# A hybrid attention and delta-rule layer: loads of the delta rule move from GpSimd's queue to SyncE's, and its first projection is issued earlier

## The chip, the cores and the metric

One core of a Trainium2 chip runs the whole layer. The metric is the device time of one execution in microseconds (us). TensorE is called PE, VectorE DVE, ScalarE ACT, GpSimd POOL and SyncE SP, as in the profile; SPq and POOLq are the DMA queues that SP and POOL issue to.

## What is computed

One layer with 512 tokens of width 2048. An input projection feeds two groups of heads, their outputs are joined and projected, and a squared-ReLU MLP follows. The change lies in the gated delta rule of the second group (8 heads, 128 wide). Cut to what matters:

```python
def hybrid_mixer(h, w_in, ...):
    proj = h @ w_in
    q_a, k_a, v_a, qkv_d, a_raw, b_raw, z = split(proj)
    attn_out = sliding_window_attention(q_a, k_a, v_a, sinks, rel_bias)   # 16 heads of 64
    qkv_d = silu(causal_depthwise_conv(qkv_d, conv_w))                    # width 4
    q_d, k_d = l2_normalise(...), l2_normalise(...)
    o_d = chunked_gated_delta_rule(q_d, k_d, v_d, g, beta)
    o_d = rms_norm(o_d) * silu(z)
    return concatenate([attn_out, o_d]) @ w_o

def chunked_gated_delta_rule(q, k, v, g, beta):
    G = cumsum(g)                                        # per chunk
    decay_mat = exp(where(tril, G[i] - G[j], -inf))
    A = strict_tril((k * beta) @ k.T * decay_mat)
    u, w = triangular_solve(A + eye, [v * beta, k * beta * exp(G)])
    attn_intra = (q @ k.T) * decay_mat
    # then a scan over the chunks with state S

def reference(x, ...):
    x = layer_norm(alpha * x + hybrid_mixer(x, ...))
    return layer_norm(alpha * x + relu(x @ w_up) ** 2 @ w_down)
```

## The kernel before

Matmuls are in fp32 by three products of high and low parts (`mul3`). Each weight block of 512 rows by 256 columns is a "unit": SP loads it (`raw`, 512 KB), ACT makes `hi` (L110), DVE makes `lo` (L111), and PE uses them. The class `Stream` keeps four raw buffers and two buffers of cut units, so the `hi` and `lo` of one unit can be written only when PE is done with the unit two before it.

`proj()` runs four units of 24 matmuls (128x512 each, tile `pj`) for two column blocks. After each of the 16 row blocks it calls `tick()`, which lets the oldest generator of `fronts` and the oldest of `chains` issue one more step. So the small work of attention heads and of the delta rule is spread between projection matmuls. First come K, V and four Q projections, each of which adds two `attend` chains (scores `ps_s` L507, softmax L513 to L528, transposes `ps_pt` L538, output `ps_o` L554). Then, after `while chains or fronts: tick()`, the attention's memory pool `at` is closed and the pool `ch` of the delta rule is opened.

The delta rule goes over four pairs of heads, called pairs 0 to 3 below. Each has three projections with a `front` (convolution `acc` L592, SiLU `s` L598, transposes `ps_tr` L604) and then one `delta` chain, which runs beside the projections of the next pair (beside the gate projections for pair 3). Of one `delta` chain these steps matter, each for the pair's two heads:

- `C` (L673): the row of cumulated decays, broadcast to 128 partitions by a DMA from DRAM; DVE subtracts (L675, 4 per head) and clips (L678), ACT takes the exponential (L679).
- `B` and `A` (L694, L698): DVE scales the products of keys by C.
- `tri` (L712): B is sent to DRAM; `Nb` (L721): its 16x16 diagonal blocks come back, one DMA per head and chunk of 128 tokens, each element apart in 64-byte rows.
- `bl` (L704): POOL masks B for the first level of the inversion.
- `dX`, `X` (L729, L731): DVE inverts all blocks by 15 steps of substitution; `inv` (L737) sends X to DRAM, and `D` (L742) loads the block-diagonal matrix back.
- `ps_z` (L757) and `ps_c` (L767): PE doubles the block size level by level, beginning with D and `bl`.

The tag C has two buffers, which the tile `zero` (L867, sent to `inv` once by POOL) shares. A scheduler decides each engine's final order from the order of the code and from dependences; each engine then works through its list in order, so an instruction that waits holds all that stand behind it on that engine or issuing queue.

Of the kernel before, what the change touches and what calls it, by code (L numbers as in the profile page):

```python
# [17 lines left out]
P = 128  # L18
# [20 lines left out]
LEVS = (4, 5)  # L39
# [15 lines left out]
def hymba_layer(ctx: ExitStack, tc: tile.TileContext, i, out, dbg=None):  # L55
    nc = tc.nc
# [42 lines left out]
    def mmbank(name):  # L99
        return mm.tile([P, 512], F32, tag="mm", name=name)  # L100
# [4 lines left out]
    def mul3(ps, wh, wl, xh, xl, start, stop, more=False):  # L105
        for a, b, first, last in ((wh, xh, start, False), (wh, xl, False, False), (wl, xh, False, stop)):
            nc.tensor.matmul(ps, a, b, start=first, stop=last, skip_group_check=more)  # L107
# [127 lines left out]
    def tick():  # L235
        for q in (fronts, chains):
            while q:
                try:
                    next(q[0])
                    break  # L240
                except StopIteration:
                    q.popleft()
# [34 lines left out]
    def proj(before=None, ticks=1):  # L277

        pss = [mmbank(f"pj{f}") for f in range(2)]
        for u in range(4):  # L280
            for k in range(4):
                kt = u * 4 + k
                if before is not None:
                    before(kt)
                if k == 0:
                    hi, lo = ws.get()
                for f in range(2):
                    fs = slice(f * P, (f + 1) * P)
                    mul3(pss[f], hi[:, k, fs], lo[:, k, fs], xH[kt], xL[kt],
                         kt == 0, kt == KT - 1)  # L290
                for _ in range(ticks):
                    tick()
        return pss
# [266 lines left out]
    for c in range(4):  # L560
# [2 lines left out]
            chains.append(attend(2 * c + f, qps[f]))  # L563
        tick()

    while chains or fronts:
        tick()
    pat.close()
# [4 lines left out]
    H2 = range(2)  # L573


    tri = dram.tile([2, P, TT * P], F32, name="tri")
    inv = dram.tile([2, P, TT * P], F32, name="inv")

    def diagonal(m, a, t):

        v = m[a, 0, t * P:t * P + 1]
        return bass.AP(v.tensor, v.offset, [[BS * TT * P + BS, P // BS], [TT * P, BS], [1, BS]])

    def t2(tag, name, bufs=None):
        return ch.tile([P, TT, P], F32, tag=tag, name=name, bufs=bufs)
# [76 lines left out]
    def delta(pr, st):  # L662
# [5 lines left out]
        C, A, B, DT, Dm = ([None] * 2 for _ in range(5))  # L668
        gv = grow.rearrange("(t h) c -> h t c", h=8)
        for a in H2:  # L670
            h = heads[a]
            C[a] = t2("C", "C")
            nc.gpsimd.dma_start(C[a], gv[h].partition_broadcast(P))  # L673
            for t in range(TT):
                nc.vector.scalar_tensor_tensor(out=C[a][:, t, :], in0=C[a][:, t, :],  # L675
                                               scalar=G_c[:, t, h:h + 1], in1=negm,
                                               op0=ALU.subtract, op1=ALU.add)
            nc.vector.tensor_scalar(out=C[a], in0=C[a], scalar1=0.0, scalar2=None, op0=ALU.min)  # L678
            nc.scalar.activation(C[a], C[a], AF.Exp)  # L679
        yield  # L680
        for a in H2:
            A[a], B[a] = t2("A", "A"), t2("B", "B")
            for th in range(2):
# [8 lines left out]
                for tt in range(2):  # L692
                    t = th * 2 + tt
# [8 lines left out]
        def masked(a, l):  # L702
            bl = t2("bl", "bl", 2)
            nc.gpsimd.tensor_tensor(out=bl, in0=B[a], in1=lev[l].unsqueeze(1).broadcast_to([P, TT, P]),  # L704
                                    op=ALU.mult)
            return bl
# [3 lines left out]
        nb_ = P // BS  # L710
        for a in H2:
            nc.gpsimd.dma_start(tri[a], B[a].rearrange("p t c -> p (t c)"))  # L712
        yield
        bls = [masked(a, LEVS[0]) for a in H2]
        yield
        Nb = ch.tile([2 * TT * nb_, BS, BS], F32, tag="Nb", name="Nb", bufs=1)
        X = ch.tile([2 * TT * nb_, BS, BS], F32, tag="X", name="X", bufs=1)
        for a in H2:
            for t in range(TT):
                p0 = (a * TT + t) * nb_  # L720
                nc.gpsimd.dma_start(Nb[p0:p0 + nb_], diagonal(tri, a, t))  # L721
        nc.scalar.activation(X, eyes, AF.Copy)
        yield
        yield
# [9 lines left out]
        for a in H2:  # L734
            for t in range(TT):
                p0 = (a * TT + t) * nb_
                nc.gpsimd.dma_start(diagonal(inv, a, t), X[p0:p0 + nb_])  # L737
        yield
        yield
        for a in H2:  # L740
# [8 lines left out]
        for l in LEVS:  # L749
# [11 lines left out]
            if l < 5:  # L761
                bls = [masked(a, l + 1) for a in H2]
# [40 lines left out]
        for t in range(TT):  # L803
            tok = slice(t * P, (t + 1) * P)
            pss, R = [None] * 2, [None] * 2
# [23 lines left out]
            for a in H2:  # L829
                h = heads[a]  # L830
# [41 lines left out]
    for pr in range(4):  # L872
        st = {"s2": [None] * 3, "K": [None] * 2, "V": [None] * 2,
              "ss": small.tile([P, 2, 2, TT], F32, tag="ss", name="ss")}
        for role in range(3):
            pss = proj()
            fronts.append(front(role, st, pss, pr))
            tick()
        chains.append(delta(pr, st))
# [192 lines left out]
    for n in range(4):  # L1072
        ns = slice(n * 512, (n + 1) * 512)
        pss = [mmbank(f"po{t}") for t in range(TT)]
# [455 lines left out]
```

## Time and profile before

| | |
|---|---|
| median of 3 runs | 2233.16 us (2230.01 to 2242.14) |
| the profiled execution's own time | 2244.22 us |
| its span in the profile | 2242.4 us |
| PE busy | 2167.1 us, 97% of the span |
| DVE, ACT, POOL busy | 65%, 44%, 16% |

The span is that of one execution, and 1.8 us of its own time lie outside it. Start times are counted from the span's start. The delta rule and the last attention heads lie between about 195 and 700 us; before that are the first projections, after it the output projection and the MLP, which the change leaves as they are.

### The profile page before, as it was taken

The numbers are of one execution on the slowest core, as the hardware profiler recorded it, in microseconds if no ns is written. First come the engines' busy times: TensorE is split into PE (matmuls) and PEld (weight loads), VectorE is DVE, ScalarE is ACT, GpSimd is POOL, SyncE is SP. The second block draws the span as 40 slices with busy tenths as digits, with TensorE's granted clock in tenths as the row PEclk, the third lists the DMA queues.
The fourth block names the chain that finished last, engine by engine and source line by source line (L and its number), as shares of the span: only waits on it lengthen the run. The fifth ranks groups of instructions, "written<-read, shape, count | busy, mean of one in ns | idle before, by whom it ended". The sixth has DMA issues, their size and how long they took to land.

```text
span 2242.4 us, 37213 instructions
## 1 busy us (share of the span) xinstructions
PE 2167.1 (97%) x15051; PEld 1986.3 (89%) x15051; DVE 1458.8 (65%) x2170; ACT 982.7 (44%) x1474; POOL 354.1 (16%) x435
## 2 busy tenths in 40 slices
PE   8999999899999999899999999999899999999996
PEld 6777788787888887799999999999899999999995
DVE  4355567565644347867656555668788788778787
ACT  3345325233333224555555555555444444444442
POOL 0122020312110000311121111110111211211113
PEclk9999999999999999899999999999999999999998
DMA  7322332323224231389898898886898888888862
GB/s 206 94 71 71 94 110 65 94 72 82 77 77 169 94 99 62 114 216 231 207 203 214 207 204 213 208 196 212 193 226 213 194 220 210 198 212 215 202 150 94
DMA packets 157480, 352.65 MB, mean 157 GB/s; under 512 B 16539, under 2 KB 84812, under 8 KB 154748
## 3 DMA queue, kind: packets, MB, share of 16 engines
q0 software_dynamic: 40000, 132.46, 32.9%
q1 hardware_dynamic: 117308, 217.82, 28.4%
q8 instruction: 118, 1.93, 0.3%
q14 instruction: 54, 0.44, 0.1%
HBM read 325.01 MB, written 24.66 MB: 156 GB/s over the span
## 4 chain that ended last, share of the span: by engine, by line
PE 71%; issue 12%; DMA 8%; DVE 5%; POOL 2%; ACT 2%; POOLq 0%; SPq 0%; DVEq 0%; ACTq 0%
PE b L107 42%; PE pj L107 16%; PE po L107 8%; DMA raw<-in_w_down_dram 2%; DMA hf<-hd 2%; DMA T<-in_w_down_dram 1%; DVE lo L111 1%; DMA C<-grow 1%; POOL raw L186 1%; DMA tri<-B 1%; PE ps_s L507 1%; PE ps_o L554 1%; DVE mix L1438 1%; PE ps_pt L538 1%; DMA g<-in_ln_dram 1%
## 5 line engine op out<-in xcount | busy, mean ns | idle before, releaser
L107 PE MATMUL b<-slot,hi 128*128 128x256 f32 x3584 | 654.9, 286 | 8.7 <-DVE slot L1040 3.3
L111 DVE TENSOR_TENSOR lo<-raw,hi 128x1024 fp32r<-128x1024 f32 x339 | 417.9, 1233 | 312.1 <-ACT hi L110 311.8
L110 ACT ACTIVATE hi<-raw 128x1024 fp32r<-128x1024 f32 x339 | 358.8, 1059 | 508.5 <-PE b L107 252.5
L107 PEld LDWEIGHTS b<-slot,hi 128*128 128x128 f32 x3584 | 557.6, 191 | 10.6 <-DVE slot L1040 4.1
L107 PE MATMUL b<-slot,lo 128*128 128x256 f32 x1792 | 508.6, 284 | 1.5 <-DVE lo L111 1.5
L107 PE MATMUL b<-hi,slot 128*128 128x256 f32 x2608 | 477.0, 283 | 8.9 <-ACT hi L110 8.9
L107 PE MATMUL pj<-slot,hi 128*128 128x512 f32 x1408 | 462.4, 405 | 0.0
L107 PEld LDWEIGHTS b<-hi,slot 128*128 128x128 f32 x2608 | 406.5, 189 | 9.9 <-ACT hi L110 9.9
L107 PE MATMUL b<-lo,slot 128*128 128x256 f32 x1304 | 368.5, 283 | 0.8 <-DVE lo L111 0.7
L107 PEld LDWEIGHTS b<-slot,lo 128*128 128x128 f32 x1792 | 343.1, 192 | 2.4 <-DVE lo L111 2.4
L107 PEld LDWEIGHTS pj<-slot,hi 128*128 128x128 f32 x1408 | 262.5, 191 | 61.6 <-issue 6.0
L107 PE MATMUL pj<-slot,lo 128*128 128x512 f32 x704 | 283.7, 403 | 6.3 <-DVE lo L111 6.2
L110 ACT ACTIVATE hi<-T 128x1024 fp32r<-128x1024 f32 x164 | 173.7, 1060 | 201.0 <-PE b L107 181.6
L111 DVE TENSOR_TENSOR lo<-T,hi 128x1024 fp32r<-128x1024 f32 x164 | 201.8, 1231 | 83.8 <-ACT hi L110 83.8
L107 PEld LDWEIGHTS b<-lo,slot 128*128 128x128 f32 x1304 | 246.8, 189 | 1.4 <-DVE lo L111 1.3
L1001 DVE TENSOR_TENSOR mix<-mix,b 128x512 f32<-128x512 f32 x223 | 152.8, 686 | 60.6 <-PE b L107 60.2
L107 PE MATMUL b<-hl,slot 128*128 128x256 f32 x1296 | 164.5, 283 | 4.3 <-DVE mix L1001 4.3
L107 PEld LDWEIGHTS pj<-slot,lo 128*128 128x128 f32 x704 | 133.7, 190 | 37.0 <-DVE lo L111 8.3
L107 PEld LDWEIGHTS b<-hl,slot 128*128 128x128 f32 x1296 | 158.8, 191 | 5.7 <-issue 4.1
L186 POOL DMA_DIRECT2D raw<-in_w_down_dram x90 | 77.9, 865 | 496.9 <-DVE lo L111 268.7
L1001 DVE TENSOR_TENSOR F<-F,b 128x512 f32<-128x512 f32 x144 | 99.1, 688 | 82.3 <-PE b L107 80.6
L107 PE MATMUL po<-hi,slot 128*128 128x512 f32 x448 | 141.0, 395 | 0.0
(265 smaller groups left out, 2149.8 us busy)
## 6 DMA issues: line engine op xcount, KB each, us to landing
raw<-in_w_down_dram POOLq DMA_DIRECT2D x90, 512.0 KB, 5.8
raw<-in_w_in_dram SPq DMA_DIRECT2D x88, 512.0 KB, 3.5
raw<-in_w_up_dram POOLq DMA_DIRECT2D x84, 512.0 KB, 6.1
T<-in_w_down_dram SPq DMA_DIRECT2D x60, 512.0 KB, 4.7
T<-in_w_up_dram SPq DMA_DIRECT2D x56, 512.0 KB, 4.9
raw<-in_w_up_dram SPq DMA_DIRECT2D x44, 512.0 KB, 4.3
raw<-in_w_down_dram SPq DMA_DIRECT2D x34, 512.0 KB, 4.5
raw<-in_w_o_dram SPq DMA_DIRECT2D x32, 512.0 KB, 3.6
```

The lines of the kernel that those rows point to most:

```text
L107: nc.tensor.matmul(ps, a, b, start=first, stop=last, skip_group_check=more)
L110: nc.scalar.activation(hi, src, AF.Copy)
L111: nc.vector.tensor_tensor(out=lo, in0=src, in1=hi.bitcast(F32), op=ALU.subtract)
L186: nc.gpsimd.dma_start(src, nxt_, accum_op=ALU.add)
L507: nc.tensor.matmul(sc, qT[hp, b * P:(b + 1) * P], kd[hp, e, b * P + k0 - 128:(b + 1) * P], start=True, stop=True)
L538: nc.tensor.transpose(pst[:, (bb * 2 + kk) * P:(bb * 2 + kk + 1) * P], lg[a][:, b, kk * P:(kk + 1) * P], ident)
L554: nc.tensor.matmul(pso[a * 64:(a + 1) * 64, b * P:(b + n) * P], vt[:, b, vf_, vh:vh + 64], pTf[:, (2 * b + 1) * P:(2 * b + 1 + n) * P], st ...
L1001: eng.tensor_tensor(out=dst, in0=p, in1=q, op=op)
L1438: nc.vector.tensor_tensor(out=yt, in0=yt, in1=g, op=ALU.mult)
```

## The change

Four edits. The DMA that fills C is issued by SP and no longer by POOL. So are the eight DMAs of a pair that fill Nb. The two first masks `bl` are written after the sends of `inv` instead of ahead of the Nb loads, and one `yield` goes. The first of the delta rule's projections is issued before the loop that drains the attention chains, not after it.

```diff
--- before.py
+++ after.py
@@ -563,6 +563,8 @@
             chains.append(attend(2 * c + f, qps[f]))
         tick()
 
+
+    pss0 = proj()
     while chains or fronts:
         tick()
     pat.close()
@@ -670,7 +672,7 @@
         for a in H2:
             h = heads[a]
             C[a] = t2("C", "C")
-            nc.gpsimd.dma_start(C[a], gv[h].partition_broadcast(P))
+            nc.sync.dma_start(C[a], gv[h].partition_broadcast(P))
             for t in range(TT):
                 nc.vector.scalar_tensor_tensor(out=C[a][:, t, :], in0=C[a][:, t, :],
                                                scalar=G_c[:, t, h:h + 1], in1=negm,
@@ -711,14 +713,12 @@
         for a in H2:
             nc.gpsimd.dma_start(tri[a], B[a].rearrange("p t c -> p (t c)"))
         yield
-        bls = [masked(a, LEVS[0]) for a in H2]
-        yield
         Nb = ch.tile([2 * TT * nb_, BS, BS], F32, tag="Nb", name="Nb", bufs=1)
         X = ch.tile([2 * TT * nb_, BS, BS], F32, tag="X", name="X", bufs=1)
         for a in H2:
             for t in range(TT):
                 p0 = (a * TT + t) * nb_
-                nc.gpsimd.dma_start(Nb[p0:p0 + nb_], diagonal(tri, a, t))
+                nc.sync.dma_start(Nb[p0:p0 + nb_], diagonal(tri, a, t))
         nc.scalar.activation(X, eyes, AF.Copy)
         yield
         yield
@@ -735,6 +735,7 @@
             for t in range(TT):
                 p0 = (a * TT + t) * nb_
                 nc.gpsimd.dma_start(diagonal(inv, a, t), X[p0:p0 + nb_])
+        bls = [masked(a, LEVS[0]) for a in H2]
         yield
         yield
         for a in H2:
@@ -873,7 +874,7 @@
         st = {"s2": [None] * 3, "K": [None] * 2, "V": [None] * 2,
               "ss": small.tile([P, 2, 2, TT], F32, tag="ss", name="ss")}
         for role in range(3):
-            pss = proj()
+            pss = proj() if pr or role else pss0
             fronts.append(front(role, st, pss, pr))
             tick()
         chains.append(delta(pr, st))
```

What the scheduler makes of it can be read from the order of instructions on the engines. Numbers of lines in the changed kernel are 1 or 2 higher behind the edits. On PE, at the last attention head: `pj_1911` and `pj_1912` are the two column blocks of the first delta projection. Before, from the first transposes to the output:

```order
L107 MATMUL pj_1912<-slot,hi 128x512 x2
L538 MATMUL ps_pt<-eye,lg 128x128
L107 MATMUL pj_1912<-slot,lo 128x512
L538 MATMUL ps_pt<-eye,lg 128x128 x2
L107 MATMUL pj_1911<-slot,hi 128x512 x2
L107 MATMUL pj_1911<-slot,lo 128x512
L107 MATMUL pj_1912<-slot,hi 128x512 x2
L107 MATMUL pj_1912<-slot,lo 128x512
L107 MATMUL pj_1911<-slot,hi 128x512
L538 MATMUL ps_pt<-eye,lg 128x128 x11
L554 MATMUL ps_o<-pT,vt 64x256 x6
L554 MATMUL ps_o<-pT,vt 64x128 x2
```

After, the same projection is `pj_1730` and `pj_1731`, and the same stretch is

```order
L538 MATMUL ps_pt<-eye,lg 128x128 x6
L107 MATMUL pj_1730<-slot,hi 128x512 x2
L107 MATMUL pj_1730<-slot,lo 128x512
L107 MATMUL pj_1731<-slot,hi 128x512 x2
L107 MATMUL pj_1731<-slot,lo 128x512
L538 MATMUL ps_pt<-eye,lg 128x128 x8
L107 MATMUL pj_1730<-slot,hi 128x512 x2
L107 MATMUL pj_1730<-slot,lo 128x512
L107 MATMUL pj_1731<-slot,hi 128x512 x2
L107 MATMUL pj_1731<-slot,lo 128x512
L554 MATMUL ps_o<-pT,vt 64x256 x6
L554 MATMUL ps_o<-pT,vt 64x128 x2
```

So the first delta projection stood between the last heads in the kernel before too, but with all scores of the last head in one block and 13 matmuls between them and the first transpose; now the scores come in two blocks with 18 matmuls behind the second, the pattern of the earlier heads. The last `ps_o` stands 6 matmuls before the end of that projection, where it stood 53 before it (both counted over the whole projection of 96).

On POOL, pair 1, from its first send on, before:

```order
L712 DMA tri<-B 128x512
L704 TENSOR_TENSOR bl<-B,cst 128x512
L673 DMA C<-grow 128x4x128
L721 DMA Nb<-tri 8x16x16 x2
L712 DMA tri<-B 128x512
L704 TENSOR_TENSOR bl<-B,cst 128x512
L721 DMA Nb<-tri 8x16x16 x6
L673 DMA C<-grow 128x4x128
L737 DMA inv<-X 8x16x16 x8
L742 DMA D<-inv 128x512 x2
```

and after:

```order
L714 DMA tri<-B 128x512
L706 TENSOR_TENSOR bl<-B,cst 128x512
L714 DMA tri<-B 128x512
L706 TENSOR_TENSOR bl<-B,cst 128x512
L737 DMA inv<-X 8x16x16 x8
L743 DMA D<-inv 128x512 x2
```

The loads of C and Nb are gone from POOL's list, and the second send of `tri` stands right behind the first mask; the masks `bl` stand behind the sends of `tri` as they did, in both kernels.

On SP, where the projections' units were one block of 80 loads before (`raw` x80), the changed list from the start of the block is:

```order
L158 DMA raw<-in_w_in_dram 128x4x256 x25
L675 DMA C<-grow 128x4x128 x2
L158 DMA raw<-in_w_in_dram 128x4x256 x9
L675 DMA C<-grow 128x4x128
L158 DMA raw<-in_w_in_dram 128x4x256
L721 DMA Nb<-tri 8x16x16 x4
L675 DMA C<-grow 128x4x128
L158 DMA raw<-in_w_in_dram 128x4x256
L721 DMA Nb<-tri 8x16x16 x4
L158 DMA raw<-in_w_in_dram 128x4x256 x10
L675 DMA C<-grow 128x4x128
```

The next rows are a unit load, the eight Nb loads of pair 1, a unit load and the second C of pair 2. The two loads of C at the top are those of pair 0 and stand behind the unit loads up to the first unit of the third delta projection. Those of pair 1 stand among the Nb loads of pair 0, those of pair 2 around the Nb loads of pair 1, each with one unit load between. DVE's list changes with it: in pairs 1 and 2 the four subtractions of the second C began behind the first `X` step of the substitution and now begin behind the third. On PE, the first `ps_z` of pair 0 comes 18 projection matmuls earlier, and those of the other pairs one or two. PE's order differs only up to the end of the delta rule; from the output projection on, every engine's list is the same but for line numbers.

## Rows read from the trace of the kernel before

**Rows 1.** The page: busy time of the engines.

```profile
PE 2167.1 (97%) x15051; PEld 1986.3 (89%) x15051; DVE 1458.8 (65%) x2170; ACT 982.7 (44%) x1474; POOL 354.1 (16%) x435
```

**Rows 2.** Waits of PE, 60 to 195 us, then 195 to 700: total, times, longest.

```profile
PE ps_G L446 <- issue: 0.3, 1, 0.3
...
PE pj L107 <- DVE lo L111: 6.2, 3, 2.4
PE ps_z L757 <- DMA D<-inv: 4.2, 2, 3.7
PE ps_tr L604 <- issue: 2.2, 1, 2.2
PE ps_pt L538 <- DVE lg L528: 2.0, 2, 1.1
```

**Rows 3.** Stretches: length; busy of PE, PEld, DVE, ACT, POOL; PEclk, DMA share, GB/s.

```profile
245.30:248.60 3.30, 3.30 (x12) 2.68 (x13) 2.00 (x4) 2.60 (x10) 0.00 (x0) 0.59 0.20 69
...
433.10:439.80 6.70, 5.14 (x17) 4.50 (x18) 1.42 (x2) 0.80 (x2) 1.85 (x2) 0.54 0.22 71
...
521.80:525.10 3.30, 3.30 (x10) 2.56 (x9) 3.30 (x8) 0.63 (x1) 0.00 (x0) 0.59 0.51 159
...
1573.10:1583.20 10.10, 5.38 (x23) 5.09 (x24) 6.48 (x7) 4.96 (x5) 1.73 (x2) 0.53 0.95 219
```

**Rows 4.** Timeline of PE: start, length, form; idle before and what ended it.

```profile
223.32 0.50 PE L107 MATMUL pj<-slot,hi 128*128 128x512 f32 x1
...
238.15 0.50 PE L107 MATMUL pj<-slot,lo 128*128 128x512 f32 x1 [1.74 <-DVE lo L111]
...
416.99 0.50 PE L107 MATMUL pj<-slot,lo 128*128 128x512 f32 x1 [2.02 <-DVE lo L111]
...
434.66 1.94 PE L757 MATMUL ps_z<-D,bl 128*128 128x64 f32 x8 [3.69 <-DMA D<-inv]
```

**Rows 5.** Timeline of POOL, first front, then pair 1.

```profile
223.95 0.80 POOL L673 DMA_DIRECT2D C<-grow  x1 [15.90 <-PE ps_o L554]
...
392.73 0.79 POOL L673 DMA_DIRECT2D C<-grow  x1
...
395.56 0.60 POOL L712 DMA_DIRECT2D tri<-B  x1 [0.76 <-DVE B L694]
...
401.43 2.37 POOL L721 DMA_DIRECT2D Nb<-tri  x4 [2.79 <-DMA tri<-B]
...
403.78 0.80 POOL L673 DMA_DIRECT2D C<-grow  x1
...
428.79 1.78 POOL L737 DMA_DIRECT2D inv<-X  x3 [2.03 <-issue]
```

**Rows 6.** Timeline of DVE, first front, then pair 1.

```profile
236.34 0.61 DVE L675 SCALAR_TENSOR_TENSOR C<-C,G_c,cst 128x128 f32<-128x128 f32 x2 [5.16 <-DMA C<-grow]
...
390.54 0.42 DVE L698 TENSOR_TENSOR A<-ps_kk,C 128x256 f32<-128x256 f32 x1
...
399.01 1.14 DVE L675 SCALAR_TENSOR_TENSOR C<-C,G_c,cst 128x128 f32<-128x128 f32 x4 [3.41 <-DMA C<-grow]
...
402.26 1.23 DVE L111 TENSOR_TENSOR lo<-raw,hi 128x1024 fp32r<-128x1024 f32 x1 [1.65 <-ACT hi L110]
...
409.68 0.35 DVE L675 SCALAR_TENSOR_TENSOR C<-C,G_c,cst 128x128 f32<-128x128 f32 x1 [2.28 <-DMA C<-grow]
...
415.72 1.21 DVE L111 TENSOR_TENSOR lo<-raw,hi 128x1024 fp32r<-128x1024 f32 x1
```

**Rows 7.** Timeline of ACT, pair 1.

```profile
411.62 0.63 ACT L679 ACTIVATE C<-C 128x512 f32<-128x512 f32 x1 [7.41 <-DVE C L678]
```

**Rows 8.** DMA issues: queue, count, size, median us to landing.

```profile
raw<-in_w_in_dram SPq DMA_DIRECT2D x88, 512.0 KB, 3.5
...
C<-grow POOLq DMA_DIRECT2D x8, 256.0 KB, 6.0
...
g<-in_ln_dram SPq DMA_DIRECT2D x8, 256.0 KB, 6.3
```

## Prediction before the changed kernel was run

> **What bounds the kernel now.** I read the page first. PE is busy for 97% of the span [rows 1], so a change that leaves PE's matmuls as they are can win only PE's idle time and the time in which its clock is low. The MLP and the output projection keep their order; what can change lies between 195 and 700 us. The second view is PE's waits in that stretch [rows 2]: 6.2 us for the low part `lo` of a weight unit (three times), 4.2 us for D, 2.2 us at a transpose `ps_tr`, 2.0 us at the transposes of the last two heads. Together 14.6 us. From 60 to 195 us, with the earlier heads, there is one wait of 0.3 us.
>
> The third view is stretches by time [rows 3]. Behind three of the waits the granted clock is not 1.00 but 0.59, 0.54 and 0.59, a mean of the two levels of 1.2 and 2.4 GHz. A stretch with busy time b at clock c lost b(1-c): 3.30x0.41 = 1.35 us, 5.14x0.46 = 2.36, 3.30x0.41 = 1.35, together 5.1. So the ceiling of this change is 14.6+5.1 = 19.7 us, 0.9%.
>
> Then I followed each wait backwards through DVE, ACT and POOL. The two largest groups have C at their head. In the first front DVE waits 5.16 us for a load of C [rows 6]; the `lo` behind it in DVE's list comes late, and PE waits 1.74 us for it [rows 4] and, one unit later, 2.2 us for `s`, which is behind it too. In pair 1 DVE waits 3.41 us for the first C of pair 2, then 2.28 us for the second [rows 6]. ACT's exponential of that C has waited 7.41 us with the next `hi` behind it [rows 7]; `lo` starts at 415.72 and PE, ready at 414.97, goes on at 416.99 [rows 4]. The same wait for the second C holds up the substitution, so `inv` and D are late and PE waits 3.69 us at `ps_z`. Pair 2 repeats this with a wait of 2.4 us for `lo` (the longest in rows 2) and none for D; pair 3 has no C to load and 4.2-3.7 = 0.5 us for D.
>
> **The change part by part.**
>
> *First projection beside the last heads.* The order shows that it stood there before too; what changes is that the last heads take the pattern of the earlier ones, 18 matmuls between scores and transposes. That pattern shows no wait for `lg` from 60 to 195 us, so the 2.0 us go. Bounds 1.5 and 2.0. Saved: 2.0.
>
> *First front.* `ps_o` of the last head ends 6 matmuls before the end of the projection instead of 53, so the pool for C opens later. A matmul takes (238.15-1.74-223.32)/55 = 0.238 us there [rows 4], the 55 being the 53 and two of the next projection. On the old time scale the projection ends at 223.32+53x0.238 = 235.9, less the 2.0 us saved 233.9; `ps_o` ends 1.4 earlier, 232.5. C was issued 0.63 us after `ps_o` [rows 4, 5], now at 233.1. With 6.0 us to land as on POOL's queue, or 6.3 as another 256 KB broadcast takes on SP's [rows 8], it is there at 239.1 to 239.4. In DVE's new list the convolution stands ahead of the Cs, and the units' `lo` too; only one subtraction of C stands ahead of the `s` that PE's transposes need. They stand 24 matmuls into the next projection, 233.9+5.7 = 239.6. After C, DVE has one subtraction (1.14/4 = 0.3) and `s`, which has half the elements of a `lo` (1.21/2 = 0.6) [rows 6], so `s` is done at about 240.0 to 240.3. I leave a wait of 0.8 us. Saved: 1.74+2.2-0.8 = 3.1, and the clock's 1.35: 4.5. Bounds: 2.0, if C lands 2 us later and the clock falls again, and 5.3.
>
> *C on SP in pairs 1 and 2.* The first C's buffer is free when `A` has read it, 390.54+0.42 = 390.96; POOL sent for the new one at 392.73, because it had a mask to do first [rows 5, 6]. On SP nothing but unit loads stands ahead. So it lands up to 1.7 us earlier, and so do the `hi`, the `lo` of 402.26 and the unit load that wait for it in turn. The second C now stands behind that unit load, and so goes out about 1.6 us before 403.78 and lands near 408.1 instead of 409.68. `lo` moves from 415.72 to about 414.1 and is done at 415.3, so PE waits 0.7 rather than 2.02, with something for jitter. Two more steps of the substitution (four instructions of 0.2 us) now stand ahead of C, so X is done 1.6+0.8 = 2.4 us earlier, and so is D. Waits for `lo` and D together shrink by these 2.4 us. POOL also paused 2.03 us between two sends of `inv` with no releaser in view [rows 5]; whether that pause is there again can't be read from the trace. I take half, 1.0. Of the clock's 2.36 us I take half, since some wait for D is left. Pair 1 saves 2.4+1.0+1.2 = 4.6. Bounds: 0 (C no earlier), and 8.1, all of it. In pair 2 the second C brings 1.5 of the 2.4 us, and 0.8 of the clock's 1.35: 2.3; bounds 0 and 3.8.
>
> *Nb on SP.* The second `tri`, sent at 395.56, stands behind a load of C and two of Nb on POOL's queue, and Nb waited for it until 401.43 [rows 5]. Without C ahead it should land sooner. Ahead of DVE's later steps stands C, so this is worth nothing in pairs 1 and 2 beyond what is counted; in pair 3, where no C is loaded, it takes away the 0.5 us for D. SP's loads of units wait behind the Nb loads until `tri` is in, a few us each time; these run ahead of their use by more than a unit (24x0.238 = 5.7 us), since four raw buffers stand against two cut ones. Cost nothing; without that cover each pair would pay what SP waits, about 2.8 us.
>
> *Masks.* POOL's list keeps them behind `tri`, so that edit does nothing.
>
> *Pair 0.* PE reaches its `ps_z` 18 matmuls, 4.3 us, earlier, while X is helped by about as much: its C steps now stand ahead. There was no wait; a new one, or small ones elsewhere, I put at 1.0 us, bounds 0 and 3.
>
> Sum: 2.0+4.5+4.6+2.3+0.5-1.0 = 12.9 us. The profiled execution took 2244.22, so 2231.3 by its own scale. It was 11.1 us above the median; much of that is one late weight load in the MLP: at 1573 us PE was busy for 5.38 of 10.10 us at clock 0.53 [rows 3], 4.7+2.5 = 7.2 us. The change doesn't touch it. On the median's scale: 2233.2-12.9 = 2220.3.
>
> **The rivals.**
>
> *C lands no sooner on SP (R1).* For it: an equal broadcast on SP's queue took 6.3 us, against 6.0 [rows 8], and each second C stands right behind a unit load of 512 KB that itself takes 3.5 us. Against: C on POOL's queue shared it with `tri` and Nb. Then pairs 1 and 2 keep only the 0.8 us from the moved steps and half a us of clock: 2.0+4.5+0.8+0.5+0.5-1.0 = 7.3, so 2226. The Trainium skill's page "DMA: Bandwidth & Descriptors", section "Issuing engines are not separate DMA queues", speaks for this one: all issuers share the same 16 DMA engines, and spreading saves only the issuer's time. By that rule the sum would be R1's. The two broadcasts of equal size, 6.0 and 6.3 us, agree; whether C loses time behind its neighbours no run here shows yet.
>
> *All of it comes back (R2).* If `s` is in time, POOL's pause goes and no stretch loses its clock: 19.7 us, 2213.5. For it: every wait has C or its order at its head. Against: D's wait in pair 1 is longer than what C gives.
>
> *Nb loads become slow on SP (R3), the other side.* They are 32 DMAs of 8 KB in 64-byte rows, which SP never issued before. If on SP's queue each took its time one after the other behind the 3.5 us of a unit load, the substitution would start late in all four pairs by L. D's lateness then goes straight to PE, with about 2.4 us of clock per pair as pair 1 paid. The savings of 6.5 us in the heads and first front stay; slower by over 11.2 us begins where 4(L+2.4) passes 17.7, L = 2.0. With L = 4 it is 25.6-6.5, so 2252. Against: nothing in the rows shows small loads queueing so, and unit loads run at 3.5 us with others in flight.
>
> **How the numbers follow.** Half a per cent, 11.2 us, is about what a measurement of this kernel tells from no change. My forecast (2214 to 2226) gets 0.50, R1 0.25, R2 0.18, R3 0.07. Faster by more than 0.5%, below 2222.0: R2 and two thirds of the forecast's case, 0.18+0.33 = 0.51. Slower: most of R3, 0.05. Within: the rest, 0.44. The likeliest case gives 2220. The range leaves out R3 and the ends of R2 and R1: 2211 to 2231.
>
> **What would show it.** Right: no wait of PE for `lg`; the wait for `lo` in the first front gone and under 1.2 us at `ps_tr`; the second C of pairs 1 and 2 landing 1 to 2 us earlier against the substitution's start; PE's wait at `ps_z` of pair 1 below 2.5 us, at pair 3 none; fewer stretches below full clock. Wrong: C on SP taking over 7 us, DVE waiting for Nb longer than before, unit loads so late that PE waits for `hi`, or a wait at `ps_z` in pairs 0 and 2.

## The result, and the profile after

| | before | after |
|---|---|---|
| median | 2233.5 us (8 runs, 2230.01 to 2242.14) | 2220.61 us (8 runs, 2216.58 to 2225.88) |
| ratio | | 0.9939, 95% interval 0.9923 to 0.9955 |
| the profiled execution | 2244.22 us | 2220.53 us |

The change takes 12.9 us off (by the interval 10 to 17), 0.6%. The page of the changed kernel, its span and its busy times:

```profile
span 2218.7 us, 37232 instructions
...
PE 2152.5 (97%) x15051; PEld 1974.7 (89%) x15051; DVE 1461.3 (66%) x2170; ACT 981.7 (44%) x1474; POOL 327.5 (15%) x395
```

PE's busy time fell with the span, by 14.6 us against [rows 1], though it runs the same 15051 matmuls. So more went than waits: part of PE's busy time before was time at a low clock or at a slower pace. Not all of the 14.6 us are the change's, though: in a second profile of the kernel before PE is busy for 2157.8 us, which leaves 5.3 (the first experiment below). PE's waits between 195 and 700 us, the answer to [rows 2]:

```profile
PE ps_z L758 <- DMA D<-inv: 3.4, 4, 1.5
PE pj L107 <- DVE lo L111: 1.0, 2, 0.5
PE ps_ot L606 <- DVE o_sb L858: 0.2, 1, 0.2
```

The 14.6 us of [rows 2] are 4.6 us now. The heads' wait for `lg` and the first front's wait at `ps_tr` are gone, the wait for `lo` fell from 6.2 to 1.0 us. D is waited for in all of pairs 1 to 3, but no longer for 3.7 us at once. The places on PE's timeline that answer to [rows 4]:

```profile
239.41 0.60 PE L606 MATMUL ps_tr<-eye,s 128*128 128x128 f32 x4
...
407.94 0.50 PE L107 MATMUL pj<-slot,lo 128*128 128x512 f32 x1 [0.51 <-DVE lo L111]
...
423.20 1.08 PE L758 MATMUL ps_z<-D,bl 128*128 128x64 f32 x8 [1.52 <-DMA D<-inv]
...
519.56 1.08 PE L758 MATMUL ps_z<-D,bl 128*128 128x64 f32 x8 [1.37 <-DMA D<-inv]
```

The first row is the first front: no wait at the transposes. Then pair 1 with 0.5 us for `lo` and 1.5 us for D, and pair 2 with 1.4 us for D (its wait for `lo` is 0.5 us too). The granted clock was 1.00 all through this stretch, where [rows 3] shows three stretches below it.

The issues of SP's queue in pair 1 (a row stands for a group, from its first start to its last end), which answer to [rows 5]:

```profile
388.95 4.61 SPq L721 DMA_DIRECT2D Nb<-tri  x8
394.25 0.40 SPq L158 DMA_DIRECT2D raw<-in_w_in_dram  x1
394.69 0.51 SPq L675 DMA_DIRECT2D C<-grow  x1
```

POOL in pair 1, the sends of `inv`:

```profile
414.25 4.78 POOL L737 DMA_DIRECT2D inv<-X  x8 [24.30 <-ACT hi L110]
```

DVE in pair 1, the answer to [rows 6]:

```profile
401.03 0.35 DVE L677 SCALAR_TENSOR_TENSOR C<-C,G_c,cst 128x128 f32<-128x128 f32 x1 [2.49 <-DMA C<-grow]
...
406.68 1.21 DVE L111 TENSOR_TENSOR lo<-raw,hi 128x1024 fp32r<-128x1024 f32 x1
```

To compare these with [rows 4 to 6], mind that this kernel is 9.05 us ahead where PE goes on after the wait for `lo` (416.99 less 407.94), and 7.5 us ahead just before, since 1.5 us of that wait were saved there. The second C goes out at 394.69, which is 1.6 us earlier against the rest than 403.78, and DVE waits 2.49 us for it, no less than before. The eight sends of `inv` go in one piece, without the pause of 2.03 us.

### The profile page after: what moved, and what is told of

It reads as the page before. It is cut to its first block, busy times and chain, and to the rows that moved or that the text cites. A ratio compares the mean times of both kernels' runs of the same rounds, so it can differ in the third digit from the quotient of the medians.

```text
span 2218.7 us, 37232 instructions
## 1 busy us (share of the span) xinstructions
PE 2152.5 (97%) x15051; PEld 1974.7 (89%) x15051; DVE 1461.3 (66%) x2170; ACT 981.7 (44%) x1474; POOL 327.5 (15%) x395
## 4 chain that ended last, share of the span: by engine, by line
PE 75%; issue 8%; DMA 7%; DVE 6%; ACT 2%; POOL 2%; SPq 0%; POOLq 0%; ACTq 0%; DVEq 0%
PE b L107 45%; PE pj L107 16%; PE po L107 8%; DMA raw<-in_w_down_dram 2%; DMA hf<-hd 2%; DVE lo L111 1%; DMA T<-in_w_down_dram 1%; PE ps_s L507 1%; ACT hi L110 1%; DVE mix L1439 1%; PE ps_o L554 1%; DMA g<-in_ln_dram 1%; DMA xc<-in_x_dram 1%; DMA C<-grow 1%; PE ps_pt L538 1%
## 5 line engine op out<-in xcount | busy, mean ns | idle before, releaser
L107 PE MATMUL b<-slot,hi 128*128 128x256 f32 x3584 | 646.7, 283 | 8.7 <-DVE slot L1041 3.3
```

## The experiments

Ratios are to the kernel before, timed on the same chip beside it, with a 95% interval. They need not equal the ratio of the two medians; where the two differ much, both are given. There were three sets of runs: the first profile again and the single edits, then C back, Nb back and the first two attempts, then the rest. The single times of the kernel before lie between 2230 and 2238 us in the first set and between 2230 and 2254 us in the other two, so there the intervals are wider.

### The kernel before, again

No edit: one more profile of it.

> The kernel before, profiled a second time, to see which of its waits stand in every execution. My theory: the waits between 195 and 700 us come from the order of instructions, so they repeat within 0.3 us each (14.6 us in all, with three stretches below full clock), while the first profile's excess over the median (2244.2 against 2233.5) lies in the MLP and is not there again: span 2229 to 2235 us. Rival: the excess lies in the delta rule's waits and was luck there, so these waits come out 5 us or more smaller this time, and part of the gain seen between the two profiles is no gain of the change.

It took 2231.99 us. PE's waits between 195 and 700 us:

```profile
PE pj L107 <- DVE lo L111: 6.7, 3, 2.4
PE ps_z L757 <- DMA D<-inv: 2.2, 3, 1.1
PE ps_pt L538 <- DVE lg L528: 2.0, 2, 1.1
PE ps_tr L604 <- issue: 0.6, 1, 0.6
```

And one of three stretches of 3.3 us at low clock, this one in pair 1 (length; busy time of PE, PEld, DVE, ACT, POOL; PEclk; DMA share; GB/s):

```profile
416.60:419.90 3.30, 3.28 (x8) 2.60 (x9) 3.30 (x10) 0.52 (x2) 0.00 (x0) 0.52 0.52 159
```

The waits for `lo` and for `lg` repeat. The wait for D came out at 2.2 us instead of 4.2, and that at `ps_tr` at 0.6 instead of 2.2. So of [rows 2] some 3 us belonged to that one execution, less than the rival's 5. In the second profile PE waits 11.5 us and loses about 3.28x0.48 = 1.6 us in each of the three stretches: 16.3 us in all. This is the better base for what the change could win: less the 4.6 us of waits that are left, it gives 11.7 us, near the 12.9 measured.

The two profiles of this kernel differ by 12.2 us. About 3 are the waits. More than half lies in the MLP, which the change doesn't touch. This is the stretch between two waits of PE there, in the first profile and in the second:

```profile
1102.30:1571.20 468.90, 466.88 (x3864) 465.52 (x3864) 297.43 (x298) 249.82 (x301) 70.95 (x82) 1.00 0.86 208
...
1097.34:1559.81 462.47, 460.35 (x3864) 459.01 (x3864) 297.27 (x298) 249.42 (x301) 70.77 (x82) 1.00 0.85 211
```

The same 3864 matmuls took 6.4 us less, and in the profile of the changed kernel they took 462.5 us as well. Of the 6.4 us, 1.7 are a stretch of 3.4 us at half clock from 1102.6 on; what slowed the rest, no run here tells. The wait for a late weight load right behind this stretch is in all three profiles: 5.9 and 6.1 us before, 6.6 us in the changed kernel.

### One edit at a time

**The first projection alone.**

```diff
+    pss0 = proj()
     while chains or fronts:
...
-            pss = proj()
+            pss = proj() if pr or role else pss0
```

> Only the first delta projection is issued ahead of the drain loop; C and Nb stay on POOL's queue. My theory: the heads' waits for lg (2.0 us) and the first front's waits for lo and the transposes with their half clock (3.9 + about 2 us) hang on this edit alone, because it moves the last output of attention and with it the place of C behind the convolution in DVE's list: 6 to 8 us less than before, ratio 0.9965 to 0.9973, and pairs 1 and 2 as before (D wait 3.7, lo waits 2.0 and 2.4). Rival: the first front needs C on SP's queue; then only the 2.0 us of the heads go and the ratio is 0.999.

Ratio 0.9976 (0.9964 to 0.9988), 2228.75 us: 5.4 us less (by the interval 3 to 8). Its waits of PE:

```profile
PE pj L107 <- DVE lo L111: 4.9, 2, 2.4
PE ps_z L758 <- DMA D<-inv: 4.0, 2, 3.5
```

The waits in the heads and the first front are gone, with C still on POOL's queue; `lo` and D in pairs 1 to 3 wait as before. The theory holds in kind; the size came out just below its 6 to 8 us, for a reason that the second profile of before shows: the first front's waits were 0.6 us at `ps_tr` and 1.9 for `lo` there, not 3.9 in all.

**C alone on SP's queue.**

```diff
-            nc.gpsimd.dma_start(C[a], gv[h].partition_broadcast(P))
+            nc.sync.dma_start(C[a], gv[h].partition_broadcast(P))
```

> Only the loads of C go by SP's queue. My theory: nothing in the heads and the first front (C's second load still waits for the zero send), and in pairs 1 and 2 the first C goes out 1.6 us earlier and with it lo and the second C: 4 to 6 us less, ratio 0.997 to 0.998. Rival one: C behind unit loads on SP's queue lands no sooner and the pairs stay as they were, ratio 0.9995 to 1.0005. Rival two: it also frees the first front, 10 us or more less.

Ratio 0.9989 (0.998 to 0.9998), 2231.32 us: 2.5 us less, and at most 4.5. Its waits:

```profile
PE pj L107 <- DVE lo L111: 4.6, 4, 1.6
PE ps_z L757 <- DMA D<-inv: 3.8, 3, 1.8
PE ps_tr L604 <- issue: 2.4, 1, 2.4
PE ps_pt L538 <- DVE lg L528: 2.0, 2, 1.1
```

The front and the heads wait as before, which refutes the second rival. The waits for `lo` shrank (the longest from 2.4 to 1.6), those for D did not go. The gain is between the theory's 4 to 6 us and the first rival's nothing. POOL in pair 1 shows what ate part of it:

```profile
394.97 1.37 POOL L721 DMA_DIRECT2D Nb<-tri  x2 [4.05 <-DMA tri<-B]
396.33 0.61 POOL L712 DMA_DIRECT2D tri<-B  x1
```

The first two Nb loads wait for the first `tri`, and the second `tri` stands behind them. It goes out 7.3 us after the first (sent at 389.06); in the kernel before it was 4.6 us (395.56 less 390.94). SP now sends C at 389.12, together with the first `tri`, which took 5.6 us to land instead of 2.3. DVE's substitution starts 16.9 us after the first `tri` where it was 14.8.

**Nb alone on SP's queue.**

```diff
-                nc.gpsimd.dma_start(Nb[p0:p0 + nb_], diagonal(tri, a, t))
+                nc.sync.dma_start(Nb[p0:p0 + nb_], diagonal(tri, a, t))
```

> Only the loads of Nb go by SP's queue. On POOL the second C of pairs 1 and 2 then stands right behind the second mask and no longer behind four Nb loads that wait for tri: it can go out about 6 us earlier (397.5 instead of 403.8 in pair 1). My prediction gave this edit 0.5 us in all; if that holds the ratio is 0.9995 to 1.0005. Rival, formed from POOL's order in the changed kernels: Nb's move is what frees the second C, the waits for lo (2.0 and 2.4 us), most of the 3.7 us for D in pair 1 and two stretches of low clock go: 7 to 9 us less, ratio 0.996 to 0.997.

Ratio 0.9974 (0.9964 to 0.9985), 2230.06 us: 5.8 us less by the ratio (3 to 8 by its interval; the medians are 3.7 us apart), in any case many times the 0.5 us that my prediction gave to this edit, and less than the rival's 7 to 9. Its waits:

```profile
PE ps_z L757 <- DMA D<-inv: 5.0, 3, 3.0
PE pj L107 <- DVE lo L111: 2.2, 3, 1.8
```

And POOL in pair 1, with one row of pair 2:

```profile
391.89 0.79 POOL L673 DMA_DIRECT2D C<-grow  x1
394.72 0.55 POOL L712 DMA_DIRECT2D tri<-B  x1 [2.04 <-DVE B L694]
...
396.53 0.78 POOL L673 DMA_DIRECT2D C<-grow  x1
...
522.36 0.60 POOL L737 DMA_DIRECT2D inv<-X  x1 [2.09 <-issue]
```

Nearly all that is left of the wait for `lo` is the first front's 1.8 us, and the wait for D in pair 1 is 1.6 us instead of 3.7. The second C goes out at 396.53, right behind the second mask, where [rows 5] has it at 403.78 behind four loads of Nb that had waited for `tri`. So the rival is shown: on POOL's list the Nb loads held C. The last row, a pause ahead of the last send of `inv` in pair 2, can account for up to 2.1 of the 3.0 us by which D is late there in this kernel; more on it below.

### The changed kernel with one edit undone

**C back on POOL's queue** (the diff of C above, the other way round).

> The changed kernel with the loads of C back on POOL's queue. Theory A, from the runs so far (first projection 5.4, Nb 5.8, C 2.5 us, which add up to the change's 13): the edits add, and this kernel stands 11 us below the one before, ratio 0.995, 2 to 3 us above the changed one; no waits for lo in pairs 1 and 2, since the second C goes out right behind the second mask, and 1.5 to 3 us for D in pairs 1 and 2. Theory B, that of my prediction: C on SP is what frees pairs 1 and 2; then 6 to 7 us of the gain go and the ratio is 0.997 with lo waits of 2 us.

Ratio 0.9965 (0.994 to 0.999). Its waits:

```profile
PE ps_z L758 <- DMA D<-inv: 5.8, 3, 2.9
PE pj L107 <- DVE lo L111: 1.0, 2, 0.8
```

The interval holds A's 0.995 and B's 0.997 alike (the medians, 2226.32 and 2237.39 us, give 0.995); the waits decide. There is 1.0 us for `lo`, no more than with C on SP, and the waits for D are 2.3 and 2.9 us in pairs 1 and 2. C on SP is not what took the waits for `lo` away.

**Nb back on POOL's queue.**

> The changed kernel with the loads of Nb back on POOL's queue. Theory A (the edits add): 8 us below the kernel before, ratio 0.9965, with the waits for lo (1.6 us) and D (1.8 and 1.5 us) that C alone on SP left. Theory B (my prediction, Nb worth 0.5 us): as the changed kernel, ratio 0.994.

Ratio 0.9996 (0.9972 to 1.002), medians 2232.82 and 2237.39 us: most of the gain is gone. Its waits:

```profile
PE ps_z L758 <- DMA D<-inv: 6.6, 3, 2.8
PE pj L107 <- DVE lo L111: 4.9, 4, 1.6
```

POOL in pair 1 of this kernel:

```profile
389.08 1.29 POOL L721 DMA_DIRECT2D Nb<-tri  x2 [3.61 <-DMA tri<-B]
390.37 0.60 POOL L714 DMA_DIRECT2D tri<-B  x1
```

B fails by size, and A's 0.9965 lies just outside the interval. Since A's terms have intervals of their own, whether the edits add can't be told from this. In pairs 1 and 2 the waits are those that A took over from C alone on SP: 1.6 us for `lo` in each, and 1.9 and 1.8 us for D. New are 2.8 us for D in pair 3, where C alone had 0.4; why, no run here tells.

The rows show the same hold as with C alone: the two Nb loads wait for the first `tri`, and the second goes out 6.8 us after it (390.37 less 383.60). The new place of the masks is not the cause, for with C alone on SP they stood in the old one and it was 7.3 us. So C's move is hampered as long as Nb is on POOL's list.

**The masks back** behind the sends of `tri`, with their `yield`.

> The changed kernel with the two first masks written behind the sends of tri again, and the yield that went with them. POOL's and SP's lists are then the same as in the changed kernel, since the scheduler puts the masks there in both; PE's and DVE's differ by a few places in pair 0's doubling steps. My theory: this edit is worth nothing, within 2 us of the changed kernel on the same chip. Rival: the yield, which lets each pair's chain run one step of 6 matmuls sooner, was worth 2 us or more.

Ratio 0.9931 (0.9905 to 0.9956), 2221.74 us, against 0.9948 (0.9924 to 0.9972) of the changed kernel timed beside it. No difference that the intervals can tell; with Nb on SP this edit is worth nothing that can be measured.

**The changed kernel again.**

> The changed kernel again, beside the others of this call. If the edits' gains simply add (5.4, 2.5 and 5.8 us when done alone), it is 12 to 15 us below the kernel before, ratio 0.9935 to 0.9945, and its profile has again 1.0 us of waits for lo, 3.4 us for D and no stretch below full clock between 195 and 700 us. Rival: that the stretches of low clock were absent was luck of one execution; then 1 to 3 stretches of 3.4 us at half clock are there behind the waits for D.

Ratio 0.9948 (0.9924 to 0.9972): the result stands, 11.6 us by these runs. But its single times go from 2218.28 to 2243.41 us, and the profiled execution was that of 2243.41. Its waits of PE:

```profile
PE ps_z L758 <- DMA D<-inv: 3.9, 3, 1.7
PE pj L107 <- DVE lo L111: 1.1, 2, 0.6
PE ps_z L758 <- PE pj L107: 0.6, 1, 0.6
```

And two stretches behind the waits for D in pairs 1 and 2:

```profile
425.10:452.20 27.10, 27.10 (x123) 23.74 (x122) 8.09 (x15) 8.88 (x29) 1.76 (x2) 0.50 0.02 4
...
534.40:561.50 27.10, 27.10 (x124) 23.73 (x123) 8.16 (x15) 8.93 (x29) 1.68 (x2) 0.50 0.02 4
```

The same stretch behind pair 1 in the first profile of the same program, with the columns:

```profile
core 0: us, PE busy (x) PEld busy (x) DVE busy (x) ACT busy (x) POOL busy (x), PEclk, DMA share, GB/s
...
425.10:452.20 27.10, 27.10 (x200) 23.56 (x199) 17.40 (x38) 13.84 (x44) 1.88 (x2) 1.00 0.10 27
```

The waits are the same as in the first profile (1.57 and 1.72 us for D at these places, against 1.52 and 1.37). Yet here PE ran 27.1 us at a clock of 0.50, twice: 123 matmuls instead of 200. Each cost 27.1x(1-123/200) = 10.4 us, together 21 of the 22.9 us between the two executions. So what a wait costs beyond itself isn't fixed: after nearly the same wait the clock stayed up once and fell for 27 us another time. The rival is shown, and larger than I had put it.

### Three attempts on what is left

**inv and D on both queues, half each.**

```diff
-                nc.gpsimd.dma_start(diagonal(inv, a, t), X[p0:p0 + nb_])
+                (nc.gpsimd if a else nc.sync).dma_start(diagonal(inv, a, t), X[p0:p0 + nb_])
...
-            nc.gpsimd.dma_start(Dm[a].rearrange("p t c -> p (t c)"), inv[a])
+            (nc.gpsimd if a else nc.sync).dma_start(Dm[a].rearrange("p t c -> p (t c)"), inv[a])
```

> The changed kernel with the sends of inv and the load of D of one head of each pair on SP's queue and those of the other on POOL's. What is left between 195 and 700 us is 3.4 us of waits for D and 1.0 us for lo. If the eight sends one after the other on POOL (4.8 us) make D late, half of them in parallel take 2.4 us off each D and 2 to 3.5 us off the time: ratio to the kernel before 0.9925. Rival: on SP the load of D stands behind a unit load that waits for lo, and the scheduler puts ps_z 6 matmuls (1.4 us) earlier, so the waits for D stay or grow: 0.994 to 0.996.

Ratio 1.0063 (1.0038 to 1.0088): 14 us slower than before. D is late now in pair 0 too, at the first `ps_z` that needs the second head:

```profile
330.17 1.20 PE L758 MATMUL ps_z<-D,bl 128*128 128x64 f32 x7 [2.64 <-DMA D<-inv]
```

The rival had the direction right, but not the size (it had 0.994 to 0.996). Most of the size is the clock's: three stretches of 24 to 27 us at half clock follow the waits in this profile, behind pairs 0, 1 and 2. The one in pair 1:

```profile
436.80:463.80 27.00, 27.00 (x125) 23.83 (x124) 5.30 (x13) 6.95 (x29) 1.28 (x1) 0.50 0.05 17
```

**The second C on POOL's queue, the first on SP's.**

```diff
-            nc.sync.dma_start(C[a], gv[h].partition_broadcast(P))
+            (nc.gpsimd if a else nc.sync).dma_start(C[a], gv[h].partition_broadcast(P))
```

> The changed kernel with the first C of each pair on SP's queue and the second on POOL's, which has nothing to do by then. The second C no longer stands behind Nb and a unit load on SP, so it goes out about 5 us earlier (390 instead of 394.7 in pair 1), DVE has no wait of 2.5 us for it, and the waits for lo (0.5 twice) and part of D's (1.5 and 1.6) go: 1 to 3 us below the changed kernel, ratio 0.9925 to 0.9935. Rival: ps_z is put 4 matmuls earlier (0.9 us) and waits for D as before: ratio 0.994.

Ratio 0.9966 (0.9941 to 0.9992); the medians, 2226.88 and 2237.39 us, give 0.995. Its waits:

```profile
PE ps_z L758 <- DMA D<-inv: 5.7, 3, 2.1
...
PE pj L107 <- DVE lo L111: 0.2, 1, 0.2
```

The waits for `lo` are down to 0.2 us, but 5.7 us for D stand in their place. The rival is nearer: in pair 1 D is there 0.8 us sooner than in the changed kernel (422.38 against 423.20), but PE is ready for it 1.1 us sooner (420.54 against 421.68).

**One send of inv per head, alone and with `ps_z` later.** `inv` is laid out so that all 32 diagonal blocks of a head lie at one stride; the second kernel adds six yields.

```diff
+    DG = P // BS * (BS * P + BS)
+    inv = dram.tile([2, TT * DG], F32, name="inv")
+    def inv_blocks(a):
+        v = inv[a, 0:1]
+        return bass.AP(v.tensor, v.offset, [[BS * P + BS, TT * P // BS], [P, BS], [1, BS]])
...
+            nc.gpsimd.dma_start(inv_blocks(a), X[p0:p0 + TT * nb_])
```

> The changed kernel with inv laid out in DRAM so that all diagonal blocks of a head lie at one stride: two sends of 32 blocks for a pair instead of eight of 8, and D comes back in pieces of 512 bytes. POOL spends 1.2 us on issuing the sends instead of 4.8, so D should be there 3 us earlier. But the scheduler also puts ps_z 16 matmuls (3.8 us) earlier. Theory: the wait for D follows the scheduler's place for ps_z and not only the time of D, so it is the same or longer (1.5 to 2.5 us for pairs 1 to 3, and one in pair 0) and the time is that of the changed kernel or up to 4 us more. Rival: D's lateness comes from the issues alone, the waits vanish and it is 3 us faster.

> The kernel with one send per head and six more yields ahead of the doubling steps, which puts ps_z 10 matmuls (2.4 us) later in pairs 1 and 2 and 36 later in pair 3, but not in pair 0. If ps_z's place against D decides, the waits for D in pairs 1 to 3 are gone, and with 1 us left for lo this is 2 to 4 us below the changed kernel, unless pair 0 (ps_z 15 matmuls earlier than in the changed kernel) now waits 1 us or more. Rival: the 512-byte pieces make D's load so much slower that the waits stay.

The first came to 1.0118 (1.008 to 1.0155), 27 us slower than before. Its waits, and one of three stretches at half clock, behind the wait in pair 2:

```profile
PE ps_z L768 <- DMA D<-inv: 9.8, 5, 2.8
PE pj L107 <- DVE lo L111: 1.1, 2, 0.6
```

```profile
533.40:563.80 30.40, 30.40 (x140) 27.13 (x140) 7.27 (x16) 8.42 (x31) 2.53 (x2) 0.50 0.07 19
```

D is waited for 9.8 us in all, as the theory had it: the scheduler's place for `ps_z` moved further than D did. In pair 1, counted from the first `tri`, D came 2.6 us sooner than in the changed kernel and PE 3.7 us. But its 4 us were far too little. Three stretches of 27 to 31 us at half clock, behind the waits of pairs 0, 2 and 3, cost most of it.

The second came to 0.9994 (0.9967 to 1.0021). Its waits:

```profile
PE ps_z L774 <- DMA D<-inv: 6.6, 4, 2.6
PE ps_tr L617 <- DVE X L742: 5.0, 3, 2.4
```

Only pair 1's wait for D is gone; pairs 2 and 3 still wait 2.2 and 1.8 us. `ps_tr` now waits for DVE's substitution in pair 1 (2.3 us, and 2.4 in pair 2), and pair 0 waits 2.6 us for D, the exception that I had named. Two stretches of 24 us at half clock follow the waits of pairs 0 and 2. None of these attempts beat the changed kernel.

## Why the prediction was right, step by step

The forecast was 2220 us and 12.9 us less; measured were 2220.6 and 12.9. The chain of waits was the right one, and so was the direction. That the size agrees to a tenth of a us is luck: two terms of wrong size offset each other.

- *Heads, 2.0 us.* Right: the wait for `lg` is gone.
- *First front, 4.5 us.* Right in mechanism: C moved behind the convolution in DVE's list, and the first projection alone did it. I left 0.8 us at `ps_tr`; there was none. With the heads, that edit alone measured 5.4 us (3 to 8) against my 6.5.
- *C on SP in pairs 1 and 2, 6.9 us.* The chain came as worked out: the second C out 1.6 us earlier, 0.5 us left for `lo` (I had 0.7), the pause on POOL gone, D's wait in pair 1 at 1.5. But I put it all down to C's queue, and C alone on SP measured 2.5 us (0.4 to 4.5). This term was too large. What it left out is that the first `tri` lands 3 us later once C is sent beside it, and that the second `tri` waits for that behind two Nb loads as long as these are on POOL's list.
- *Nb on SP, 0.5 us.* This is the term that was mis-sized: 5.8 us alone (3 to 8), and without it most of the gain goes (the interval leaves at most 6 us of it). I looked at what Nb waited for and not at what stood behind it on POOL's list. The row was there: in [rows 5] the four Nb loads wait until 401.43, and the second C follows at 403.78 and no sooner. With Nb off that list, C or `tri` go out at once; with C off it as well, `tri` has the queue to itself.
- *Masks, nothing.* Right as far as it was tried: undone in the changed kernel it made no difference that the intervals can tell. With Nb on POOL it was not tried by itself.
- *Pair 0 and others, minus 1.0.* In the first profile no wait at pair 0's `ps_z`, in the second 0.55 us, with the masks back 2.3. About right.
- *Clock.* I charged each stretch as [rows 3] showed it, 1.35 to 2.36 us, and left about half of two. In the first profile of after none was left; in the second two of 27 us stood in the same places. The price was taken from one execution and is no constant.
- *The profile against the median.* That the first profile's excess is not the change's is borne out for the most part: the second took 2231.99 us, 12 us less, of which 3 us were waits in the delta rule. But the late weight load at 1573 us, to which I gave 7.2 us of the excess, is hardly part of it: PE's wait there is in the second profile and after the change too (5.9 us, then 6.1 and 6.6). What went is 6.4 us of slower running ahead of it.

R1 (C no sooner) was right about the landing: on SP's queue the second C took 6.3 us, from 394.69 to 401.03, as long as on POOL's. It was wrong about the time, because the issue came earlier. R3 did not happen: DVE waited 3.1 us for Nb in all instead of 8.9.

## What to carry to other kernels

When an instruction waits in an in-order list, price first what stands behind it; here moving the loads that waited was worth 5.8 us (3 to 8), because of the load behind them. Undo edits as well as doing them alone: without Nb's move the other three together came to a ratio of 0.9996 (0.9972 to 1.002), so a gain can hang on the edit that was thought to be worth next to nothing. And a wait of PE of 1.5 us ahead of a stretch of small matmuls can cost 1.5 or 12 us from one execution to the next, so take such a wait away rather than halve it, and read its price from more than one profile.

## What the runs showed of the hardware that I had not expected

**The clock after a wait.** Behind a wait of 1.5 to 2.8 us for D the granted clock was 1.00 throughout (1.5 us in the first profile of after, and 2.6 us in pair 1 with one send per head), 0.50 for 3.4 us (1.8 us with the second C on POOL), or 0.50 for 24 to 31 us. So the length of the wait doesn't decide. The long ones began 0.3 to 2.4 us after the wait and went on through the doubling steps with their 64-column matmuls. In the second profile of after one lasted from 425.0 to 452.3; the doubling steps ended at 448.7, and 512-column matmuls followed. It is not the chip alone: the twelve executions of the changed kernel in its second run were all on one, took 2218 to 2243 us, and had a mean granted clock of 0.990 down to 0.978, the longest time with the lowest clock. What makes one execution fall and another not, no run here tells.

**Two transfers at once.** Where SP sends C within 0.1 us of POOL's first `tri`, that `tri` took 5.5 us to land in pair 1 (changed kernel; 5.2 with Nb back on POOL, 5.6 with C alone on SP). With C on POOL's queue, sent 1.8 us behind it, it took 2.3 us, in the kernel before and with C back on POOL. Whether the queue or the time of sending does it, no run here separates. So moving C has a price that the prediction didn't have.

**A pause of POOL.** The pause of 2 us ahead of a DMA issue is no accident of one execution. In the second profile of before it stands at the same instruction, the sixth send of `inv` in pair 1:

```profile
428.42 1.77 POOL L737 DMA_DIRECT2D inv<-X  x3 [2.04 <-issue]
```

So it does with the first projection alone. With Nb on SP it stands at the eighth send of pair 2 (522.36, above), the same with C back on POOL, and with the second C on POOL at the sixth send of pair 3:

```profile
607.09 1.78 POOL L737 DMA_DIRECT2D inv<-X  x3 [2.14 <-issue]
```

With C alone on SP, and with Nb back on POOL, it stands at the eighth Nb load of pair 2 (2.4 us in both). The fewer instructions POOL has, the later it comes, and in the changed kernel, which has the fewest of these, it is at none of these sends. It goes with POOL's list of instructions, not with the work at that place; its cause was not tried.
